# A chunked RWKV-7 recurrence on TensorE: half-array products per head made into full-array products for both heads

## The chip, the cores and the metric

The kernel runs on one core of a Trainium2 chip, in fp32. The metric is device time in microseconds (us) for one execution; lower is better. The engines are named as in the profile: PE (TensorE, matrix products; PEld is its weight load), DVE (VectorE), ACT (ScalarE), POOL (GpSimd) and SP (SyncE, which issues most transfers).

## The reference, cut to what matters

One decoder layer over 512 prompt tokens and 8 decode rows, model width 2048. A combined input projection feeds a gMLP branch and an RWKV-7 branch; both are gated, projected, merged and projected out. The part that the change touches is the recurrence of 32 heads of size 64:

```python
def step(s, inp):
    r_t, w_t, k_t, v_t, a_t, b_t = inp
    sa = jnp.einsum('bhij,bhj->bhi', s, a_t)
    s = s * w_t[:, :, None, :] + sa[..., None] * b_t[:, :, None, :] + v_t[..., None] * k_t[:, :, None, :]
    y_t = jnp.einsum('bhij,bhj->bhi', s, r_t)
    return s, y_t
...
proj = jnp.einsum('btd,de->bte', h, w_in)
...
s_new, y = _wkv_scan(wkv0, r_h, w_h, k_h, v_h, -kk, kk * a_h)
```

The kernel computes it in 8 chunks of 64 tokens: inside a chunk everything is matrix products and the inverse of a triangular 64 x 64 matrix, and the 64 x 64 state of each head goes from chunk to chunk.

## The kernel before, in words

**Main stream.** `emit_pe` writes one long stream of products of 128 x 128 weights with 260 columns: each addend pair costs three PE instructions (`acc<-hh,hi`, `acc<-hl,hi`, `acc<-hh,lo`), since weights and activations are split in a high and a low part. After each such triple it calls `side.tick()`, and there the side work may put in its own instructions. I call the place after a triple a slot.

**Side work.** Every instruction passes through the wrapper `Engine.call`, so all rows carry its line, L130, and are told apart by their tiles. `Side` holds generators. A planner (`Engine.cost`) estimates each engine's clock, and a bare `yield` means "go on when what this step started should be done, at the next slot". So the order on every engine is fixed when the program is built; on the chip, semaphores make an engine wait where the estimate was too short. `side.drain(t)` advances the planner without main products until task t is done.

**A pair of heads.** There are 16 pairs (two heads: partitions 0 to 63 and 64 to 127). The main stream has three or four input-projection jobs a pair, plus one more job in even pairs, 9 jobs (288 slots) in two pairs. `pair_task(p)` starts when k of pair p has been projected, and makes the token factors (`GGt`, `LK`), the products `gram`, the inverses of 32 x 32 blocks on POOL (tile `mtm`), and then the 64 x 64 inverses `MT`. `pair_aux(p)` makes `TK` (transposed factors) and `X` (token-major v, with room for the state). Then comes the chain of 8 chunks, one pair at a time (`lock["chain"]`), and a group norm. `pre_pair(p)` drains task p - 4 before pair p is projected.

**A chunk.** In lines 1086 to 1126, with h the head: product `R` (two products with 64 output partitions, K = 128), the part of `y` from X (two), a copy `rs` on DVE, product `U` with the inverse (two, K = 64), two copies into X on DVE, product `S` (two) and the second part of `y` (two, K = 64), then two adds on DVE that make the next state in X. An fp32 product is two PE instructions, so a chunk is 20 PE instructions in three groups: R with y, U, and S with y.

**The inverse.** Lines 1031 to 1080: blocks go from POOL through a DRAM tile (`md`) into `MT`, a fresh tile for each pair, with SP's transfers; a yield of 4500 ns; two DVE transposes (`m11tb`); the products `t` and `m`; copies; then the chain may begin.

Of the kernel before, what the change touches and what calls it, by code (L numbers as in the profile page):

```python
# [9 lines left out]
OP = mybir.AluOpType  # L10
# [86 lines left out]
class Both:  # L97
    """Two tiles indexed as one along their second dimension."""
# [8 lines left out]
class Engine:  # L107
    """An engine whose instructions are counted on the estimated clock."""
# [57 lines left out]
def hybrid_step(ctx, tc, xT, cT, wc, vecs, sst, win, wlr, w2a2, stw, lnv, wsT, w00, bs, pa, pb, wo,  # L166
# [7 lines left out]
    # ---------------------------------------------------------------- pools  # L174
# [49 lines left out]
    # ---------------------------------------------------------------- constants  # L224
# [4 lines left out]
    c9 = C((128, KD, 9), "c9")  # L229
    SY.dma_start(out=vec, in_=vecs)  # L230
    SY.dma_start(out=c9, in_=cT)

    open_pool("h", "h", "right")
    hs = slots("h", 32)
    open_pool("g", "gel")
    NG_S = 21
    gs = slots("g", NG_S)
    lp = open_pool("lead", "lead")
    xt = [hs(name="x") for _ in range(KD - 1)] + [lp.tile([128, N], F32, name="x15")]
# [22 lines left out]
    bones = C((128, 128), "bones")  # L262
# [3 lines left out]
    vmat = C((128, 128), "vmat")  # L266
    V.tensor_scalar(vmat, bones, 1.0 / 64, None, OP.mult)
    cmat = C((128, 128), "cmat")
# [29 lines left out]
    cpad = C((128, KD, 32), "cpad")  # L298
# [130 lines left out]
    # ---------------------------------------------------------------- conditioning, norm, h  # L429
# [26 lines left out]
    def cond_pair(g0, g1, tile_of, tmp, c0=0, w=256, kt=0):  # L456
        """w columns of c @ w_c + b_c from each of two column groups, features on partitions."""
# [73 lines left out]
    # ---------------------------------------------------------------- gMLP branch  # L531
# [219 lines left out]
    # ---------------------------------------------------------------- RWKV branch  # L751
    NW_S = 39
    ws = slots("wkv", NW_S)
    lora = {}
    pair = [dict() for _ in range(HP)]
# [5 lines left out]
    def pre_rwkv():  # L761
        side.drain(mix_task["g"])
        cur["gm"].release()
        cur["g"].release()
        open_pool("wkv", "wkv")
        load_lora(0)
# [61 lines left out]

    def parts(t):
        """The two addends of t that the tensor engine takes in one pass each."""  # L830
# [5 lines left out]
    def pair_aux(p):  # L836
        """What the chunks need besides the inverses: token-major v, b and k; the bonus; decode columns."""
# [43 lines left out]
        X = [ws((128, NCH, 64), name="x") for _ in range(2)]  # L881
        for cg in range(2):
# [3 lines left out]
            for c in range(4):  # L886
                o = 4 * cg + c
                if o < 7:
                    PE.transpose(ps[:, 128 * c:128 * c + 128], v[:, 64 * o:64 * o + 128], ident)
                    continue  # L890
                for h in range(2):
                    t = 64 * (7 * h)
                    PE.matmul(p3[hx[1 - h], c, 64 * h:64 * h + 64], v[hx[h], t:t + 64],
                              ident[hx[h], 64 * h:64 * h + 64], start=True, stop=True)
            yield
            A.copy(X[1][hx[0], 4 * cg:4 * cg + 4, :], p3[hx[0], :, 64:128])
            n = 4 - cg
            A.copy(X[0][hx[1], 4 * cg + 1:4 * cg + 1 + n, :], p3[hx[1], 0:n, 0:64])
            if cg:
                A.copy(X[0][hx[1], 0, :], p3[hx[1], 3, 0:64])  # L900
            give()
            yield
        for h in range(2):
            V.memset(X[h][hx[h], 0, :], 0.0)
# [3 lines left out]
    def pair_task(p):  # L908
# [5 lines left out]
        # squared norm of kk, decay, in-context rate  # L914
# [55 lines left out]
        del inv, f  # L970
        yield
        # token factors, scaled by the cumulated decay
        GGt = [[ws((128, 4, 128), name="gg") for _ in range(2)] for _ in range(2)]
# [6 lines left out]
        for cg in range(2):  # L980
            cc = slice(4 * cg, 4 * cg + 4)
            for h in range(2):
                x = hx[h]
                gg = GGt[h][cg]
                V.scalar_tensor_tensor(gg[x, :, 0:64], c3(k)[x, cc], vec[x, V_KK + p:V_KK + p + 1], pt[x, cc, 0:64],
                                       OP.mult, OP.mult)
                V.tensor_tensor(gg[x, :, 64:128], c3(r)[x, cc], pt[x, cc, 1:65], OP.mult)
# [5 lines left out]
            for c in range(4):  # L993
                for h in range(2):
                    PE.matmul(gr[h][:, 128 * c:128 * c + 128], LK[cg][hx[h], c, :], GGt[h][cg][hx[h], c, :],
# [12 lines left out]
            for h in range(2):  # L1008
                y = hx[1 - h]
                V.tensor_tensor(GGt[h][cg][y], g3[h][y], mask[y].unsqueeze(1).to_broadcast([64, 4, 128]), OP.mult)  # L1010
                give()
        del ip, pt
        aux = side.add(pair_aux(p))
        # inverses of the 32 x 32 diagonal blocks, one block on four partitions
# [28 lines left out]
        for h in range(2):  # L1043
            z = slice(64 * h, 64 * h + 32)
            V.transpose(M11[z], MT[z, :, 0:32])
# [19 lines left out]
        for c in range(NCH):  # L1065
            for h in range(2):
                z, y = slice(64 * h, 64 * h + 32), slice(64 * h + 32, 64 * h + 64)
                PE.matmul(p3[z, c, :], tb[y, c, :], MT[y, c, 32:64], start=True, stop=True)
# [3 lines left out]
        for h in range(2):  # L1072
            z = slice(64 * h, 64 * h + 32)
            V.tensor_copy(MT[z, :, 32:64], p3[z])
# [5 lines left out]
        del LK  # L1080
        # the chunks, one after another
# [4 lines left out]
        for c in range(NCH):  # L1086
            cg, c4 = c // 4, c % 4
            R = psum("ch", 1, "R")
            for h in range(2):
                PE.matmul(R[hx[h], 0:64], GGt[h][cg][:, c4, 0:64], X[h][:, c, :], start=True, stop=True)  # L1090
            for h in range(2):
                PE.matmul(py[hx[h], 64 * c:64 * c + 64], X[h][:, c, :], GGt[h][cg][:, c4, 64:128],
                          start=True, stop=False)
            if c:
                sp = wk.tile([128, 64], F32, tag="sp", bufs=2, name="sp")
                for h in range(2):
                    A.activation(sp[hx[h]], X[h][hx[h], c, :], AF.Identity, scale=pc[hx[h], c, :])
            yield
            rs = wk.tile([128, 64], F32, tag="rs", bufs=2, name="rs")
            V.tensor_copy(rs, R[:, 0:64])  # L1100
            yield
            U = psum("ch", 1, "U")
            for h in range(2):
                PE.matmul(U[hx[h], 0:64], MT[hx[h], c, :], rs[hx[h]], start=True, stop=True)
            yield
            for h in range(2):
                V.tensor_copy(X[h][hx[h], c, :], U[hx[h], 0:64])
            yield
            S = psum("ch", 1, "S")
            for h in range(2):  # L1110
# [5 lines left out]
            if c == NCH - 1:  # L1116
                sf = wk.tile([128, 64], F32, tag="sf", bufs=1, name="sf")
                V.tensor_tensor(sf, S[:, 0:64], sp, OP.add)
                G.dma_start(out=wkvp[p], in_=sf)
            else:  # L1120
                for h in range(2):
                    if c:
                        V.tensor_tensor(X[h][hx[h], c + 1, :], S[hx[h], 0:64], sp[hx[h]], OP.add)
                    else:
                        V.tensor_copy(X[h][hx[h], c + 1, :], S[hx[h], 0:64])
            yield
        lock["chain"] = None
        del X, GGt, BB, TK, MT
        # group norm
# [91 lines left out]
    # ---------------------------------------------------------------- decode rows of the WKV state  # L1221
    def sample_task():
# [71 lines left out]
        bc = lambda t, n: t.unsqueeze(2).to_broadcast([128, HP, n])  # noqa: E731  # L1294
# [18 lines left out]
    # ---------------------------------------------------------------- merge  # L1313
# [5 lines left out]
    def load_ya():  # L1319
        """All of y_a is loaded, and the tiles for which the slots suffice split, before the merge begins."""  # L1320
# [20 lines left out]
    def load_yb():  # L1341
# [7 lines left out]
        for p in range(HP):  # L1349
# [4 lines left out]
            hi, lo = ws(dt=F32R, name="ybh"), ws(dt=F32R, name="ybl")  # L1354
# [63 lines left out]
    # ---------------------------------------------------------------- output projection, residual, final norm  # L1418
# [176 lines left out]
```

## Time and profile before

| what | us |
|---|---|
| median of 3 runs (2405.62 to 2407.21) | 2406.22 |
| span of the profiled execution | 2405.5 |
| PE busy | 2365.4 (98%) |
| DVE busy | 1445.9 (60%) |
| ACT busy | 936.8 (39%) |
| POOL busy | 572.0 (24%) |

The profiled execution is told by its span, which lies 0.7 us under the median of the runs; the profile gives nothing else around it. PE products overlap in their pipeline, so the busy time of a group of them is no price: what a product costs the stream is read from the starts of its neighbours.

### The profile page before, as it was taken

The page shows a single profiled execution, that of the slowest core. Times are in us where ns is not written, and L with a number is a line of the kernel's source. Part 1 is how long each engine was busy: PE and PEld are TensorE (multiplying, and loading weights), DVE is VectorE, ACT ScalarE, POOL GpSimd, SP SyncE. Part 2 cuts the span into 40 slices and gives each one's busy share as a digit, 9 for nine tenths or more (in the row PEclk, how much of TensorE's full clock was granted, in tenths as well). Part 3 has the DMA queues.
Part 4 walks back from the last instruction along what each step waited for, and adds up shares of the span by engine and source line. Part 5 has one row for each costly group of instructions (what it writes and reads, how often), then busy time and mean ns, then how long its engine had stood idle before and what let it go on. Part 6 is the DMA issues. An engine that isn't in the chain of part 4 may idle for free.

```text
span 2405.5 us, 54026 instructions
## 1 busy us (share of the span) xinstructions
PE 2365.4 (98%) x22155; PEld 2222.8 (92%) x22155; DVE 1445.9 (60%) x3091; ACT 936.8 (39%) x2033; POOL 572.0 (24%) x1371
## 2 busy tenths in 40 slices
PE   8999999999999999999999999999999999999997
PEld 6899999999889989999899998998989999999996
DVE  6655452337667757776677666776678753434435
ACT  4333421243434454454544444444423342223333
POOL 3410011004322343323423244233512150000001
PEclk9999999999999999999999999999999999999998
DMA  8764267322222222222223232222234654334235
GB/s 291 278 228 150 97 209 244 104 94 88 89 86 83 85 75 88 87 75 84 83 80 96 66 92 79 85 87 68 96 127 162 215 187 137 119 120 172 88 97 142
DMA packets 165544, 296.73 MB, mean 123 GB/s; under 512 B 69192, under 2 KB 86344, under 8 KB 164656
## 3 DMA queue, kind: packets, MB, share of 16 engines
q1 hardware_dynamic: 149616, 239.13, 32.1%
q0 software_dynamic: 15680, 54.16, 6.1%
q8 instruction: 173, 2.83, 0.5%
q14 instruction: 75, 0.61, 0.1%
HBM read 264.94 MB, written 28.28 MB: 122 GB/s over the span
## 4 chain that ended last, share of the span: by engine, by line
PE 93%; issue 2%; POOL 2%; DMA 1%; DVE 1%; ACT 0%; SPq 0%; DVEq 0%; POOLq 0%; ACTq 0%
PE acc L130 77%; PE y L130 2%; PE m L130 2%; PE gram L130 2%; PE R L130 1%; PE S L130 1%; PE U L130 1%; POOL mtm L130 1%; PE lora L130 1%; PE vT L130 1%; DMA wcr<-in_wc 1%; PE tk L130 1%; PE t L130 0%; PE bon L130 0%; PE gnv L130 0%
## 5 line engine op out<-in xcount | busy, mean ns | idle before, releaser
L130 PE MATMUL acc<-hh,hi 128*128 128x260 f32 (+1 forms) x3904 | 1164.3, 298 | 2.9 <-DVE gel L130 1.8
L130 PE MATMUL acc<-hl,hi 128*128 128x260 f32 (+1 forms) x3904 | 1105.0, 283 | 0.3 <-DVE hl L130 0.3
L130 PE MATMUL acc<-hh,lo 128*128 128x260 f32 (+1 forms) x3904 | 1104.2, 283 | 0.4 <-DVE lo L130 0.4
L130 PEld LDWEIGHTS acc<-hh,hi 128*128 128x128 f32 (+1 forms) x3904 | 735.2, 188 | 48.3 <-issue 10.9
L130 PEld LDWEIGHTS acc<-hl,hi 128*128 128x128 f32 (+1 forms) x3904 | 736.5, 189 | 2.0 <-DVE hl L130 0.6
L130 PEld LDWEIGHTS acc<-hh,lo 128*128 128x128 f32 (+1 forms) x3904 | 735.8, 188 | 0.6 <-DVE lo L130 0.6
L130 DVE TENSOR_TENSOR lo<-raw,hi 128x512 fp32r<-128x512 f32 (+2 forms) x682 | 474.2, 703 | 269.6 <-ACT hi L130 265.7
L130 ACT CAST hi<-raw 128x512 fp32r<-128x512 f32 (+2 forms) x692 | 402.4, 597 | 305.9 <-PE acc L130 289.8
L130 POOL TENSOR_TENSOR mtm<-xm,mtm 128x60 f32<-128x60 f32 (+24 forms) x496 | 168.5, 340 | 223.4 <-DMA xm<-xd 187.3
L130 POOL TENSOR_TENSOR mtm<-mtm 128x60 f32<-128x60 f32 (+24 forms) x496 | 170.7, 344 | 38.8
L130 ACT ACTIVATE sp<-x,pc 64x64 f32<-64x64 f32 x224 | 77.3, 345 | 177.5 <-DVE x L130 175.1
L130 PE MATMUL acc<-mh,hi 128*128 128x260 f32 x512 | 144.8, 283 | 0.0
L130 PE MATMUL acc<-ybh,hi 128*128 128x260 f32 x512 | 144.8, 283 | 0.0
L130 PE MATMUL acc<-ybl,hi 128*128 128x260 f32 x512 | 144.6, 282 | 0.0
L130 PE MATMUL acc<-ybh,lo 128*128 128x260 f32 x512 | 144.6, 282 | 0.0
L130 PE MATMUL acc<-ml,hi 128*128 128x260 f32 x512 | 144.4, 282 | 0.0
L130 PE MATMUL acc<-mh,lo 128*128 128x260 f32 x512 | 144.2, 282 | 0.0
L130 DVE TENSOR_TENSOR gel<-gel,acc 128x260 f32<-128x260 f32 x160 | 65.2, 421 | 76.5 <-PE acc L130 76.0
L130 POOL DMA_DIRECT2D out<-xo x4 | 3.1, 771 | 421.2 <-DVE gs L130 413.4
L130 PEld LDWEIGHTS acc<-mh,lo 128*128 128x128 f32 x512 | 96.4, 188 | 0.0
L130 PEld LDWEIGHTS acc<-ybl,hi 128*128 128x128 f32 x512 | 96.4, 188 | 0.0
L130 PEld LDWEIGHTS acc<-mh,hi 128*128 128x128 f32 x512 | 96.4, 188 | 0.0
(281 smaller groups left out, 3330.0 us busy)
## 6 DMA issues: line engine op xcount, KB each, us to landing
raw<-in_win SPq DMA_DIRECT2D x240, 512.0 KB, 3.8
wcr<-in_wc POOLq DMA_DIRECT2D x57, 512.0 KB, 8.0
raw<-in_wo SPq DMA_DIRECT2D x38, 512.0 KB, 3.7
wcg<-in_wc SPq DMA_DIRECT2D x64, 256.0 KB, 5.5
raw<-in_pb SPq DMA_DIRECT2D x32, 512.0 KB, 3.8
xm<-xd SPq DMA_DIRECT2D x64, 128.0 KB, 2.7
raw<-in_pa SPq DMA_DIRECT2D x16, 512.0 KB, 3.7
x<-in_xT SPq DMA_DIRECT2D x16, 260.0 KB, 5.2
```

Of the source, the lines that this page charges most:

```text
L130: return f(*a, **k)
```

## The change

Only the recurrence and what feeds it are changed; comments are dropped, and a few constant tiles (`c9`, `cpad`, `bones`, `vmat`, `cmat`) move from the constant pool to pools that are released early.

- `GGt` (one tile for each head and half) becomes `GG` (one for each half, both heads side by side), `X` likewise holds both heads side by side, and `MT` is one 128 x 128 block-diagonal matrix for a chunk, in one tile for all pairs, zeroed once.
- R, U and S are one full-array product each. R and S have 128 columns, of which the diagonal 64 x 64 blocks are read; U has 64 columns.
- `rs` is two DVE copies, not one. U goes to a new tile `xu`, whose other half is copied from X on POOL twice every four chunks.
- The y products are held back and issued for four chunks together.
- GG waits until the chain of pair p - 2 is done, and the loads of MT until that of pair p - 1 is (`chain_passed`). Slots: `NW_S` 39 to 31, and five double-width tiles (tag D).
- The transposes of v take the first and last chunk together (`ends`), so that no half-array product remains there.

```diff
+    def wide(name, dt=F32, n=1024):
+        return cur["wkv"].tile([128, 2 * N], dt, tag="D", bufs=5, name=name)[:, 0:n]
+    def chain_passed(p):
+        while chain["done"] <= p:
+            yield "t"
...
+        yield from chain_passed(p - 2)
+        GG = [wide("gg").rearrange("p (c q h t) -> p c q h t", c=4, q=2, h=2) for _ in range(2)]
...
-        MT = ws((128, NCH, 64), name="MT")
+        yield from chain_passed(p - 1)
+        MT = chain["mt"]
         for q in range(4):
-            SY.dma_start(out=MT[32 * q:32 * q + 32, :, 32 * (q % 2):32 * (q % 2) + 32],
+            SY.dma_start(out=MT[32 * q:32 * q + 32, :, 32 * q:32 * q + 32],
                          in_=md[8 * q:8 * q + 8].rearrange("c j t -> j c t"))
-        for h in range(2):
-            V.memset(MT[64 * h + 32:64 * h + 64, :, 0:32], 0.0)
         yield 4500.0
...
+            if c4 == 0:
+                xu = ws((128, 4, 2, 64), name="xu")
+                for h in range(2):
+                    G.tensor_copy(xu[hx[1 - h], :, h, :], x[hx[1 - h], :, h, :])
             R = psum("ch", 1, "R")
-            for h in range(2):
-                PE.matmul(R[hx[h], 0:64], GGt[h][cg][:, c4, 0:64], X[h][:, c, :], start=True, stop=True)
-            for h in range(2):
-                PE.matmul(py[hx[h], 64 * c:64 * c + 64], X[h][:, c, :], GGt[h][cg][:, c4, 64:128],
-                          start=True, stop=False)
+            PE.matmul(R[:, 0:128], GG[cg][:, c4, 0], x[:, c4], start=True, stop=True)
...
-            V.tensor_copy(rs, R[:, 0:64])
+            for h in range(2):
+                V.tensor_copy(rs[hx[h]], R[hx[h], 64 * h:64 * h + 64])
...
-            for h in range(2):
-                PE.matmul(U[hx[h], 0:64], MT[hx[h], c, :], rs[hx[h]], start=True, stop=True)
+            PE.matmul(U[:, 0:64], MT[:, c, :], rs, start=True, stop=True)
...
-            for h in range(2):
-                PE.matmul(S[hx[h], 0:64], TK[cg][:, c4, 64 * h:64 * h + 64], X[h][:, c, :], start=True, stop=True)
-            for h in range(2):
-                PE.matmul(py[hx[h], 64 * c:64 * c + 64], X[h][hx[h], c, :], BB[cg][hx[h], c4, 64:128],
-                          start=False, stop=True)
+            PE.matmul(S[:, 0:128], TK[cg][:, c4, :], xu[:, c4], start=True, stop=True)
...
+            if c4 == 3:
+                for i in range(4):
+                    for h in range(2):
+                        PE.matmul(py[hx[h], 64 * (4 * cg + i):64 * (4 * cg + i) + 64], x[:, i, h, :],
+                                  GG[cg][:, i, 1, h, :], start=(c == 3 and i == 0), stop=False)
+                for i in range(4):
+                    for h in range(2):
+                        PE.matmul(py[hx[h], 64 * (4 * cg + i):64 * (4 * cg + i) + 64], xu[hx[h], i, h, :],
+                                  BB[cg][hx[h], i, 64:128], start=False, stop=(c == NCH - 1 and i == 3))
+        chain["done"] = p + 1
```

## Rows read from the trace of the kernel before

**Rows 1.** The page, parts 1 and 2: busy time of each engine with its share of the span and its instructions, and the granted clock of PE in 40 slices (9 is 90% or more of full speed).
```profile
PE 2365.4 (98%) x22155; PEld 2222.8 (92%) x22155; DVE 1445.9 (60%) x3091; ACT 936.8 (39%) x2033; POOL 572.0 (24%) x1371
...
PEclk9999999999999999999999999999999999999998
```

**Rows 2.** Busy time of each engine in a stretch of two pairs (us; the clock is the granted one).
```profile
910.50:1062.70 152.20, 152.20 (x1465) 137.95 (x1464) 105.74 (x245) 70.94 (x164) 52.05 (x145) 1.00 0.28 83
```

**Rows 3.** Timeline of PE around the three groups of a chunk: start and duration in us, what it writes and reads, how many instructions.
```profile
1000.05 0.28 PE L130 MATMUL acc<-hh,lo 128*128 128x260 f32 x1
1000.26 0.33 PE L130 MATMUL U<-rs,MT 64*64 64x64 f32 x4
1000.53 0.39 PE L130 MATMUL acc<-hh,hi 128*128 128x260 f32 x1
1000.75 0.28 PE L130 MATMUL acc<-hl,hi 128*128 128x260 f32 x1
...
1001.95 0.28 PE L130 MATMUL acc<-hh,lo 128*128 128x260 f32 x1
1002.16 0.34 PE L130 MATMUL S<-x,tk 128*64 128x64 f32 x4
1002.42 0.33 PE L130 MATMUL y<-bb,x 64*64 64x64 f32 x4
1002.68 0.39 PE L130 MATMUL acc<-hh,hi 128*128 128x260 f32 x1
1002.91 0.29 PE L130 MATMUL acc<-hl,hi 128*128 128x260 f32 x1
1003.03 0.29 PE L130 MATMUL acc<-hh,lo 128*128 128x260 f32 x1
...
1006.26 0.28 PE L130 MATMUL acc<-hh,lo 128*128 128x260 f32 x1
1006.48 0.34 PE L130 MATMUL R<-x,gg 128*64 128x64 f32 x4
1006.64 0.29 PE L130 MATMUL y<-gg,x 128*64 128x64 f32 x4
1006.86 0.39 PE L130 MATMUL acc<-hh,hi 128*128 128x260 f32 x1
1007.08 0.28 PE L130 MATMUL acc<-hl,hi 128*128 128x260 f32 x1
```

**Rows 4.** Timeline of PE earlier, in the gMLP branch, around one full-array fp32 product of 128 columns (tile mix; two instructions).
```profile
337.90 0.28 PE L130 MATMUL acc<-hh,lo 128*128 128x260 f32 x1
338.02 0.38 PE L130 MATMUL mix<-wst,vt 128*128 128x128 f32 x2
338.16 0.37 PE L130 MATMUL acc<-hh,hi 128*128 128x260 f32 x1
338.37 0.28 PE L130 MATMUL acc<-hl,hi 128*128 128x260 f32 x1
```

**Rows 5.** Groups of PE instructions over the whole span, by shape: count, then busy us and mean ns of one, then idle time before them.
```profile
L130 PE MATMUL R<-x,gg 128*64 128x64 f32 x512 | 43.1, 247 | 0.0
...
L130 PE MATMUL vT<-ident,sh 64*64 64x64 f32 x64 | 5.3, 243 | 0.0
```

**Rows 6.** Timelines of PE and of DVE in a chunk whose steps follow at the least distance, two slots.
```profile
1020.58 0.33 PE L130 MATMUL U<-rs,MT 64*64 64x64 f32 x4
1021.75 0.34 PE L130 MATMUL S<-x,tk 128*64 128x64 f32 x4
...
1021.02 0.47 DVE L130 COPY x<-U 64x64 f32<-64x64 f32 x2 [1.15 <-PE U L130]
```

**Rows 7.** Timelines of PE, SP, DVE, POOL and ACT: first R and last S of the chains of pairs 4 and 5, the load of pair 5's MT and its use, the last instruction of task 5, and the last evacuation before pair 9 is projected. Last, from the list of transfers, the median time from issue to landing (us) of the loads of MT.
```profile
909.70 0.34 PE L130 MATMUL R<-x,gg 128*64 128x64 f32 x4
...
975.75 0.34 PE L130 MATMUL S<-x,tk 128*64 128x64 f32 x4
...
975.39 1.82 SPq L130 DMA_DIRECT2D MT<-md  x4
...
985.63 0.89 DVE L130 STREAM_TRANSPOSE m11tb<-MT 32x256 f32<-32x256 f32 x2
...
996.74 0.34 PE L130 MATMUL R<-x,gg 128*64 128x64 f32 x4
...
1043.76 0.34 PE L130 MATMUL S<-x,tk 128*64 128x64 f32 x4
...
1074.70 0.56 POOL L130 DMA_DIRECT2D yb<-yc  x1 [2.05 <-DVE yc L130]
...
1144.89 0.39 ACT L130 ACTIVATE zth<-acc 128x260 f32<-128x260 f32 x1 [1.04 <-PE acc L130]
...
MT<-md SPq DMA_DIRECT2D x64, 32.0 KB, 1.9
```

**Rows 8.** PE's waits on the transposes of MT (us in total, times, longest), and two prices: the copy rs on DVE and a copy on POOL (count, busy us and mean ns of one, idle time before).
```profile
PE t L130 <- DVE m11tb L130: 3.6, 2, 3.4
...
L130 DVE COPY rs<-R 128x64 f32<-128x64 f32 x16 | 3.6, 223 | 4.1 <-PE R L130 4.0
...
L130 POOL COPY mtm<-inv 128x256 f32<-128x256 f32 x16 | 8.1, 508 | 2.1 <-DMA md<-mtm 2.1
```

More of the change, by code (lines that the diff above doesn't have):

```diff
@@ L228, in hybrid_step @@
     vec = C((128, V_N), "vec")
-    c9 = C((128, KD, 9), "c9")
     SY.dma_start(out=vec, in_=vecs)
-    SY.dma_start(out=c9, in_=cT)
     open_pool("h", "h", "right")
     hs = slots("h", 32)
-    open_pool("g", "gel")
+    gelp = open_pool("g", "gel")
     NG_S = 21
     gs = slots("g", NG_S)
+    cpad = gelp.tile([128, KD, 32], F32, name="cpad")
     lp = open_pool("lead", "lead")
+    c9 = lp.tile([128, KD, 9], F32, name="c9")
+    SY.dma_start(out=c9, in_=cT)
     xt = [hs(name="x") for _ in range(KD - 1)] + [lp.tile([128, N], F32, name="x15")]
@@ L261, in hybrid_step @@
     V.memset(ones, 1.0)
-    bones = C((128, 128), "bones")
+    bones = lp.tile([128, 128], F32, name="bones")
     V.memset(bones, 0.0)
@@ L749, in hybrid_step @@
         job(win[16 + m], 16, 128, mov_h, evac_z(m))
-    NW_S = 39
+    NW_S = 31
     ws = slots("wkv", NW_S)
     lora = {}
+    chain = {"done": 0}
     pair = [dict() for _ in range(HP)]
@@ L765, in pre_rwkv @@
         open_pool("wkv", "wkv")
+        chain["mt"] = wide("MT").rearrange("p (c t) -> p c t", c=NCH)
+        V.memset(chain["mt"], 0.0)
         load_lora(0)
@@ L880, in pair_aux @@
         collected.add(p)
-        X = [ws((128, NCH, 64), name="x") for _ in range(2)]
+        X = [ws((128, 4, 2, 64), name="x") for _ in range(2)]
+        ends = cur["wkv"].tile([128, 2, 64], F32, tag="ends", bufs=1, name="ends")
+        A.copy(ends, c3(v)[:, ::-7, :])
         for cg in range(2):
@@ L887, in pair_aux @@
                 o = 4 * cg + c
-                if o < 7:
-                    PE.transpose(ps[:, 128 * c:128 * c + 128], v[:, 64 * o:64 * o + 128], ident)
-                    continue
-                for h in range(2):
-                    t = 64 * (7 * h)
-                    PE.matmul(p3[hx[1 - h], c, 64 * h:64 * h + 64], v[hx[h], t:t + 64],
-                              ident[hx[h], 64 * h:64 * h + 64], start=True, stop=True)
-            yield
[L896 to L900, printed above, removed]
+                PE.transpose(ps[:, 128 * c:128 * c + 128],
+                             v[:, 64 * o:64 * o + 128] if o < 7 else ends.rearrange("p a b -> p (a b)"), ident)
+            yield
+            A.copy(X[cg][hx[0], :, 1, :], p3[hx[0], :, 64:128])
+            A.copy(X[cg][hx[1], 1:4, 0, :], p3[hx[1], 0:3, 0:64])
+            A.copy(X[1 - cg][hx[1], 0, 0, :], p3[hx[1], 3, 0:64])
             give()
@@ L903, in pair_aux @@
         for h in range(2):
-            V.memset(X[h][hx[h], 0, :], 0.0)
+            V.memset(X[0][hx[h], 0, h, :], 0.0)
         d["X"] = X
@@ L969, in pair_task @@
         d["b"], d["k2"] = b, k2
-        del inv, f
+        del inv, f, thw, g, tha
         yield
-        GGt = [[ws((128, 4, 128), name="gg") for _ in range(2)] for _ in range(2)]
+        yield from chain_passed(p - 2)
+        GG = [wide("gg").rearrange("p (c q h t) -> p c q h t", c=4, q=2, h=2) for _ in range(2)]
         LK = [ws((128, 4, 128), name="lk") for _ in range(2)]
@@ L1009, in pair_task @@
                 y = hx[1 - h]
-                V.tensor_tensor(GGt[h][cg][y], g3[h][y], mask[y].unsqueeze(1).to_broadcast([64, 4, 128]), OP.mult)
+                V.tensor_tensor(GG[cg][y, :, :, h, :], g3[h][y].rearrange("p c (q t) -> p c q t", q=2),
+                                mask[y].rearrange("p (q t) -> p q t", q=2).unsqueeze(1).to_broadcast([64, 4, 2, 64]),
+                                OP.mult)
                 give()
-        del ip, pt
+        del ip, pt, gg, r, k, b, k2, LK
         aux = side.add(pair_aux(p))
@@ L1044, in pair_task @@
             z = slice(64 * h, 64 * h + 32)
-            V.transpose(M11[z], MT[z, :, 0:32])
+            V.transpose(M11[z], MT[z, :, 64 * h:64 * h + 32])
         yield
@@ L1067, in pair_task @@
                 z, y = slice(64 * h, 64 * h + 32), slice(64 * h + 32, 64 * h + 64)
-                PE.matmul(p3[z, c, :], tb[y, c, :], MT[y, c, 32:64], start=True, stop=True)
+                PE.matmul(p3[z, c, :], tb[y, c, :], MT[y, c, 64 * h + 32:64 * h + 64], start=True, stop=True)
             if c == SPLIT:
@@ L1079, in pair_task @@
         X, TK = d.pop("X"), d.pop("TK")
-        del LK
         while lock["chain"] is not None:
@@ L1115, in pair_task @@
-            yield
[L1116 to L1125, printed above, removed]
@@ L1126, in pair_task @@
-            yield
+                o = S[hx[h], 64 * h:64 * h + 64]
+                if c == NCH - 1:
+                    if h == 0:
+                        sf = wk.tile([128, 64], F32, tag="sf", bufs=1, name="sf")
+                    V.tensor_tensor(sf[hx[h]], o, sp[hx[h]], OP.add)
+                elif c:
+                    V.tensor_tensor(X[(c + 1) // 4][hx[h], (c + 1) % 4, h, :], o, sp[hx[h]], OP.add)
+                else:
+                    V.tensor_copy(x[hx[h], 1, h, :], o)
+            if c == NCH - 1:
+                G.dma_start(out=wkvp[p], in_=sf)
@@ L1353, in load_yb @@
             yield 1500.0
-            hi, lo = ws(dt=F32R, name="ybh"), ws(dt=F32R, name="ybl")
+            if p < 5:
+                w = wide("ybw", F32R, 2 * N)
+                hi, lo = w[:, 0:N], w[:, N:2 * N]
+            else:
+                hi, lo = ws(dt=F32R, name="ybh"), ws(dt=F32R, name="ybl")
             A.copy(hi, t)
```

23 lines of the change are left out of this document (12 added, 11 removed).

## The prediction

> **What bounds the kernel now.** I read the page first: PE is busy for 98% of the span at full clock in almost every slice, DVE 60%, POOL 24% [rows 1]. Then I read the stretch of two pairs, where the change lives: PE is busy for all of its 152.20 us, DVE for 105.74, ACT for 70.94, POOL for 52.05 [rows 2]. So PE sets the pace, and what counts is how far apart the chain's products push the main products. The busy time of a group of products cannot be used, since they overlap; the starts can. The timeline gives them [rows 3]: two main products that follow each other start 0.12 us apart (1002.91, 1003.03). Where side products stand between, I take the distance from the last main product before to the second one after (the first one after still carries part of the delay) and subtract two plain steps, 0.24 us. That is the price of a group.
>
> **Prices before** [rows 3]. U: 1000.05 to 1000.75 is 0.70, so 0.46 for four small instructions. R with y: 1006.26 to 1007.08 is 0.82, so 0.58 for eight. S with y: 1001.95 to 1002.91 is 0.96, so 0.72 for eight of two shapes. Together 1.76 us a chunk; R has 512 instructions, four a chunk, so there are 128 chunks [rows 5], and the chain costs PE 225.3 us. These prices also show where the time goes. Four more instructions of the same shape add 0.58 - 0.46 = 0.12; four more of another shape (128 rows, then 64 rows) add 0.72 - 0.46 = 0.26. So of U's 0.46 only 0.12 is the products, and 0.34 is going from full-array to small products and back.
>
> **Prices after.** Before has a full-array fp32 product of 128 columns amid main products, mix [rows 4]: 337.90 to 338.37 is 0.47, so 0.23 for its two instructions, with no going over and back. R and S are this form exactly. U has the same weights and half the columns; no row has it, so I bound it by 0.12 (half) and 0.23, and take 0.23, because the same 128 x 128 weights have to be loaded twice. A chunk's three products then cost 0.69, and 128 of them 88.3 us. The y products stay small, 32 instructions for four chunks, 16 of each shape: the first four 0.46, twelve more of that shape 0.36, four of the other shape 0.26, twelve more 0.36, in sum 1.44 us, and 32 such batches 46.1 us. No row shows so long a batch; its upper bound is each further four at 0.26, 0.84 us more a batch or 27 us in all. The chain then costs 134.4 us, 90.9 less than before.
>
> The transposes of v: 64 small instructions [rows 5], four a pair, fall away, and one full transpose a pair takes their place. At U's 0.46 against one pass like half a mix product, 0.11, this is 0.35 a pair and 5.5 us. The sum for PE is 96.4 us: span 2405.5 - 96.4 = 2309.1.
>
> **A rule that speaks against it.** The rows price the full array at 0.23 against 0.12 for two small products inside a run of small ones. The Trainium skill, TensorEngine Tiling (Array Packing), section Theoretical Speedup, says that splitting the array pays up to 2x where a dimension is 64 or less, which is what before does and the change undoes. By that rule alone R, U and S would each be dearer by 0.11. The same page, section Key Properties, says that changing the tiling mode drains the engine; the trace agrees with this, and 0.34 is what it shows for one way in and out. I take the rows' sum; the other is a rival below.
>
> **What is given back on PE.** The order is fixed by the planner, which goes by slots, so the chain's steps keep about their distance in slots while the products between get shorter. In the tightest steps U at 1020.58 is followed by S at 1021.75, two slots later; the copies of U ran from 1021.02 to 1021.49, so S had 0.26 us to spare [rows 6]. U and S shrink to 0.23 each, which takes 0.46 - 0.23 = 0.23 from that step: it just fits, or waits some hundredths. For R the second copy rs, 0.22 more [rows 8], comes on top of 0.58 - 0.23 = 0.35, though the planner knows of the copy and may leave another slot. Bounds: nothing, or 0.1 us in each of some nine such steps a pair, 14 us. I take 5, since most steps are longer than two slots.
>
> **DVE, POOL, ACT.** One copy more a chunk is 128 x 0.22 = 28 us on DVE, less the 32 memsets of MT that go, 7 us at the copy's price. In two pairs that makes DVE about 108 us out of some 140: still under PE. The four copies a pair on POOL are 64 x 0.51 = 33 us by the nearest copy [rows 8], on an engine with two thirds of its time free [rows 2]. They stand behind inverse steps in POOL's queue, and S of chunks 0 and 4 needs them; R, rs, U and U's copies come first and cover some 2 us (U to S alone is 1.17 [rows 6]). If that cover is gone each costs up to 1 us, in the planner's slots rather than in stalls. Costed at nothing. The moved constants and the memset of MT stand outside this stretch or happen once: nothing.
>
> **The new waits.** GG waits for the chain of pair p - 2 and MT for that of p - 1. Before, MT of pair 5 was loaded from 975.39, while chain 4's last S stood at 975.75, and DVE transposed it only at 985.63 [rows 7]. After, the four loads go into SP's queue behind chain 4's end: 1.8 us of issue and 1.9 to land make about 980.5 with a us for the last adds, 5 us before use. Behind them on SP are weight loads, which before already waited longer behind the write of md. What is late next: if the chain ends 5 us later against the inverse, the transposes wait on DVE, and products t behind them on PE. Before shows two such waits, 3.6 us together, the longest 3.4 [rows 8]. Bounds: nothing, or 3.4 in each of 15 pairs, 51 us; nearest to the rows is a small part of it, and I take 0.6 a pair, 9 us.
>
> Is the chain itself fast enough? Chain 4 lasted 975.75 - 909.70 = 66.1 us, chain 5 1043.76 - 996.74 = 47.0 [rows 7], 56.5 on average. After, the least gap between chains is issue and landing of MT, 3.7, and from its transposes to the first R, 996.74 - 985.63 = 11.1, so 14.8. The second rs adds 8 x 0.22 = 1.8, the POOL copies about 2, and eight chunks lose 0.7 us of products each, 5.7. The cycle is 56.5 + 14.8 + 1.8 + 2 - 5.7 = 69.4 us. The main stream gives a pair every 76.1 - 96.4/16 = 70.1. It fits barely, so I forecast no queue of chains.
>
> **The sum:** 2309.1 + 5 + 9 = 2323.1 for the span, with 0.7 around it 2323.8 against the median of 2406.22.
>
> **Rivals.**
>
> *All is hidden.* No step waits, MT always lands in time, and U costs half: 2309.1 + 0.7 = 2309.8, or 14 us less with U at 0.12, 2296. For it: before, PE hardly ever waits in this stretch. Against it: that 0.26 us to spare is used up.
>
> *The chain falls behind.* If the cycle is longer than 70.1 us, chains fall back pair by pair. Main products stall when task p is not done as pair p + 4 begins. Task 5's last instruction stands at 1074.70 and pair 9 begins at about 1144.9 [rows 7], so 70 us can be used up, 4.7 a pair over 15 pairs. A cycle of 77 would cost 15 x 6.9 - 70 = 34 us, and DVE and PE would wait on MT in every pair, up to 51 us: 2345 to 2405. For it: 69.4 against 70.1 is close, and even chains are 66 us long. Against it: the long chains are long because they wait for other work at the planner's leisure.
>
> *The chain becomes the bound, and the kernel slower.* The same mechanism, from the point where it costs more than 97 us: a cycle above 70.1 + (70 + 97)/15 = 81.2 us, so 12 more than I work out. At 83 the time is about 2434. It would need chains longer by a fifth; nothing in rows 7 shows that.
>
> *The small products were the cheaper form.* By the tiling rule: if going over and back were not what the 0.34 is, and the interruption cost the same with full-array products, the three would be dearer by 128 x 3 x 0.11 = 42 us: 2448. The mix row speaks against it, since it is an interruption too and costs 0.23 in all [rows 4].
>
> **Chances and range.** My forecast (2308 to 2345) 0.62; all hidden (below 2308) 0.13; the chain falls behind (2345 to 2401) 0.17, of which the last bit, 0.02, counts as no change; slower by the chain 0.05; slower by the small products 0.03. No measurement of this kernel tells less than 0.2%, 5 us, from no change. So faster 0.90, same 0.02, slower 0.08. The range leaves out the lower half of the hidden case (0.06), the upper third of the chain's (0.06) and both slower ones (0.08): 2302 to 2385.
>
> **What would show it.** In the trace after: R, U and S with 128 rows and 128 columns, 256 instructions each, and main products 0.47 us apart around a lone R; y in runs of 32, near 1.7 us from main to second main; two pairs in about 140 us; DVE's transposes of MT at times waiting for its load; PE's waits on DVE in the chain, some 15 us where there were almost none. I am wrong if PE's busy rows show other prices, or if the time between two R of chunk 0 is more than two pairs' main products take, with PE idle at the start of a pair.

## The result

The changed kernel takes 2346.66 us (median of 4 runs, 2345.44 to 2347.86), the kernel before in the same series 2405.92 (2404.52 to 2407.21): ratio 0.9756, 95% interval 0.9743 to 0.977. The forecast was faster, and the range 2302 to 2385 holds the time; the likeliest value, 2323.8, is 23 us too low. So some 59 us came of 82 forecast, and the question is where the other 23 are.

The page after, parts 1, 2 and 4 (the last is the chain that ended last, by engine), against [rows 1]:
```profile
PE 2294.7 (98%) x21339; PEld 2212.8 (94%) x21339; DVE 1481.9 (63%) x3204; ACT 944.3 (40%) x2065; POOL 612.0 (26%) x1435
...
PEclk9999999999999999999999999999999999999998
...
PE 85%; DVE 6%; issue 5%; DMA 2%; POOL 2%; ACT 1%; SPq 0%; DVEq 0%; POOLq 0%; ACTq 0%
```
Two stretches of two pairs, against [rows 2] (us; busy time of PE, PEld, DVE, ACT, POOL; granted clock):
```profile
1186.10:1330.90 144.80, 143.43 (x1363) 137.24 (x1363) 109.80 (x256) 71.70 (x168) 57.56 (x153) 1.00 0.28 85
1330.90:1475.60 144.70, 143.31 (x1363) 137.06 (x1362) 110.99 (x260) 71.71 (x168) 57.91 (x153) 1.00 0.30 87
```
Two pairs take 144.75 us (144.5 on average from first R to first R), not the 140 forecast and not the 152.2 of before. And PE, which was busy for all of the stretch before, now has 1.4 us of holes in each.

Timelines of PE around a lone S and around a batch of y, against [rows 3]:
```profile
1306.05 0.28 PE L130 MATMUL acc<-hh,lo 128*128 128x260 f32 x1
1306.17 0.38 PE L130 MATMUL S<-xu,tk 128*128 128x128 f32 x2
1306.31 0.37 PE L130 MATMUL acc<-hh,hi 128*128 128x260 f32 x1
1306.51 0.29 PE L130 MATMUL acc<-hl,hi 128*128 128x260 f32 x1
...
1366.56 0.28 PE L130 MATMUL acc<-hh,lo 128*128 128x260 f32 x1
1366.77 0.69 PE L130 MATMUL y<-gg,x 128*64 128x64 f32 x16
1367.39 0.68 PE L130 MATMUL y<-bb,xu 64*64 64x64 f32 x16
1368.00 0.39 PE L130 MATMUL acc<-hh,hi 128*128 128x260 f32 x1
1368.22 0.28 PE L130 MATMUL acc<-hl,hi 128*128 128x260 f32 x1
```
From main to second main, less 0.24: S 0.46 - 0.24 = 0.22, the batch 1.66 - 0.24 = 1.42. These are the prices forecast (0.23 and 1.44). So the prices are right where nothing waits. PE's waits now have rows for the chain that before had none (us in total, times, longest), and the one on MT's transposes against [rows 8]:
```profile
PE U L130 <- DVE rs L130: 7.3, 13, 1.1
...
PE R L130 <- DVE x L130: 1.7, 3, 1.2
PE S L130 <- DVE xu L130: 1.5, 8, 0.2
...
PE t L130 <- DVE m11tb L130: 0.4, 2, 0.2
```
The rows of waits hold only the holes that show between modelled ends, 10.5 us. Starts say more. Two main products start 0.12 apart though each is drawn 0.28 long, so a start that comes 0.15 late leaves no hole. I took, for each R, U and S, its start less the start before it less the plain step (0.12; ahead of the small products of before 0.21), and added up what is over 0.02 us. Before, that is 0.1 us in the whole span. After, it is 7.0 for R (36 of 128), 14.0 for U (50) and 8.1 for S (61): 29.2 us in 147 late starts.

The longest show where they come from. PE, then DVE, around a U:
```profile
1228.14 0.38 PE L130 MATMUL R<-x,gg 128*128 128x128 f32 x2
...
1228.96 0.28 PE L130 MATMUL acc<-hh,lo 128*128 128x260 f32 x1
1230.29 0.41 PE L130 MATMUL U<-rs,MT 128*128 128x64 f32 x2 [1.05 <-DVE rs L130]
...
1228.57 1.22 DVE L130 TENSOR_TENSOR_SCAN cs<-smask,thw 128x512 f32<-128x512 f32 x1
1229.71 0.43 DVE L130 COPY rs<-R 64x64 f32<-64x64 f32 x2
```
R is done early enough, but DVE is in a scan, the two copies rs stand behind it, and U, whose turn in PE's queue was 1229.08, waits until 1230.29; all of PE's queue waits with it. The planner's formula for DVE, 80 + 1.04 ns an element, prices the scan at 612 ns, lo at 612 and a copy of 64 columns at 147; in the trace they take 1238, 717 and 220. By what DVE did just ahead of the copies, the late starts over 0.1 us (83 cases, 25.6 us) are 7.5 us behind a lo (25 cases), 6.5 behind a scan (10), the rest scattered over DVE's other instructions; in only 5 cases was DVE idle just before.

A product that waits loses more than the wait. PE's weight loads and products around an S that waited (the S of 1306.17 above, which did not, had its load at 1306.06):
```profile
1310.36 0.28 PE L130 MATMUL acc<-hh,lo 128*128 128x260 f32 x1
1310.83 0.46 PE L130 MATMUL S<-xu,tk 128*128 128x128 f32 x2 [0.19 <-DVE xu L130]
1311.04 0.36 PE L130 MATMUL acc<-hh,hi 128*128 128x260 f32 x1
1311.24 0.28 PE L130 MATMUL acc<-hl,hi 128*128 128x260 f32 x1
...
1310.80 0.30 PEld L130 LDWEIGHTS S<-xu,tk 128*128 128x128 f32 x2 [0.36 <-PE acc L130]
```
The weights (tk, long there) are loaded only after the wait, 0.03 us ahead of the product instead of 0.11, and from S to the second main product it is 0.41 instead of 0.34. Over all R, U and S that stand alone between main products, the median of this distance is 0.42 for the 133 late ones and 0.34 for the others. The Trainium skill, TensorE: Matmul & The Clock Gate, section Step-by-step: what each phase is for, says that weight loads are pulled ahead of products in flight; the S of 1306.17 agrees, the waiting S shows none of it.

### The profile page after: what moved, and what is told of

It reads as the page before. It is cut to its first block, busy times and chain, and to the rows that moved or that the text cites. A ratio compares the mean times of both kernels' runs of the same rounds, so it can differ in the third digit from the quotient of the medians.

```text
span 2346.0 us, 52985 instructions
## 1 busy us (share of the span) xinstructions
PE 2294.7 (98%) x21339; PEld 2212.8 (94%) x21339; DVE 1481.9 (63%) x3204; ACT 944.3 (40%) x2065; POOL 612.0 (26%) x1435
## 4 chain that ended last, share of the span: by engine, by line
PE 85%; DVE 6%; issue 5%; DMA 2%; POOL 2%; ACT 1%; SPq 0%; DVEq 0%; POOLq 0%; ACTq 0%
PE acc L130 71%; PE gram L130 2%; PE y L130 2%; PE m L130 2%; PE S L130 1%; PE R L130 1%; PE U L130 1%; DMA wcr<-in_wc 1%; DVE lo L130 1%; PE lora L130 1%; POOL mtm L130 1%; PE tk L130 1%; DVE cs L130 1%; DVE inv L130 1%; POOL x L130 0%
## 5 line engine op out<-in xcount | busy, mean ns | idle before, releaser
L130 POOL TENSOR_TENSOR mtm<-xm,mtm 128x60 f32<-128x60 f32 (+24 forms) x496 | 173.3, 349 | 190.5 <-DMA xm<-xd 155.5
L130 POOL TENSOR_TENSOR mtm<-mtm 128x60 f32<-128x60 f32 (+24 forms) x496 | 179.5, 362 | 38.9
L130 PE MATMUL acc<-ybl,hi 128*128 128x260 f32 x352 | 99.5, 283 | 0.0
L130 PE MATMUL acc<-ybh,hi 128*128 128x260 f32 x352 | 99.4, 282 | 0.0
L130 PE MATMUL acc<-ybh,lo 128*128 128x260 f32 x352 | 99.0, 281 | 0.0
L130 PEld LDWEIGHTS acc<-ml,hi 128*128 128x128 f32 x512 | 96.4, 188 | 0.0
```

Of the source, the lines that this page charges most:

```text
L130: return f(*a, **k)
```

## The experiments

The theory after the result: the waits of R, U and S on DVE, with these late loads, are what the forecast lacked, some 40 us. Rivals: the array form costs more than its lone price, VectorE is short whatever the chain does, or the chain is too slow for the pairs. In the diffs, the lines with + are the experiment's. Medians are held against 2346.7 for the changed kernel; brackets are the ratio to the kernel before with its 95% interval.

**The chain without its waits, first try (chain_unwaited).** Products read a constant, and the three results have columns of their own in one bank; `plan` tells the planner the old operand, so that the order stays.
```diff
+        ch = psum("ch", 1, "ch")
...
-            R = psum("ch", 1, "R")
-            PE.matmul(R[:, 0:128], GG[cg][:, c4, 0], x[:, c4], start=True, stop=True)
+            R = ch[:, 0:128]
+            PE.matmul(R, GG[cg][:, c4, 0], ident, start=True, stop=True, plan=[x])
```


> The changed kernel in which R, U and S read a constant 128x128 array as their moving operand instead of x, rs and xu, each from its own columns of one PSUM bank; the copies on the vector engine, the y products, the number of products, their shapes and their order are those of the changed kernel. So the state recurrence is left out, and no product of the chain waits for a copy. Theory (the vector engine's queue, longer than the planner's prices, makes the chain's products wait on TensorE): the starts lost in the changed kernel add up to 29 us, and each product that waited also lost some 0.1 us because its weights were loaded only after the wait: 30 to 40 us faster than the changed kernel, 2307 to 2317 us. Rival 1 (the array-shaped products simply cost more than the 0.23 us I took): the same products at the same places cost the same, 2340 to 2347. Rival 2 (VectorE is short in any case, and a TensorE that doesn't wait here waits for the operands of the main products instead): 2330 to 2347, with waits for lo in the place of those for rs, x and xu.

Measured: 2342.61 [0.9742, 0.9727 to 0.9756]. This settles nothing: the products still waited for the copies out of the one bank that all three write (6.6 us on rs in the rows of waits, against 7.3; late starts 21.9 us), though U now reads nothing of rs and writes other columns than rs reads. What it shows is that sharing one tile in one bank is enough to keep the wait.

**The chain without its waits (chain_apart).** Now the copies do not read the bank either.
```diff
-                V.tensor_copy(rs[hx[h]], R[hx[h], 64 * h:64 * h + 64])
+                V.tensor_copy(rs[hx[h]], ident[hx[h], 64 * h:64 * h + 64], plan=[R])
-            PE.matmul(U[:, 0:64], MT[:, c, :], rs, start=True, stop=True)
+            PE.matmul(U[:, 0:64], MT[:, c, :], ident[:, 0:64], start=True, stop=True, plan=[rs])
```


> The changed kernel in which TensorE and VectorE no longer meet in the recurrence: R, U and S read a constant 128x128 array as their moving operand, and the copies and adds behind them read the same constant instead of R, U and S. Count, shape and order of the products and copies are those of the changed kernel; the state recurrence is left out. In the run before this one R, U and S still waited, since they wrote a bank that the copies had yet to read; here neither engine waits for the other. Theory (the waits of R, U and S for VectorE, 29 us of late starts and some 0.1 us more for each product that waited, are what the forecast missed): 30 to 40 us under the changed kernel, 2307 to 2317 us, with the price of a lone S at 0.23 instead of 0.32 us. Rival 1 (the array-shaped products, or what stands around them, cost more than I took): 2335 to 2347, with the prices as they were. Rival 2 (VectorE is short, and the main products wait for lo instead): 2325 to 2347, with a wait for lo of over 5 us.

Measured: 2307.05 [0.9597, 0.9583 to 0.9611], 39.6 us under the changed kernel. No start of R, U or S is late, a lone one costs 0.22 each, and the two stretches of two pairs, in the same columns:
```profile
1168.30:1308.20 139.90, 139.90 (x1360) 135.63 (x1359) 109.20 (x259) 71.27 (x169) 57.77 (x152) 1.00 0.30 90
1308.20:1448.40 140.20, 140.20 (x1362) 135.92 (x1361) 110.06 (x259) 71.52 (x169) 59.01 (x153) 1.00 0.30 90
```
PE is busy for all of it, and two pairs take the 140 forecast. PE, DVE, ACT and POOL run the same instructions in the same order as in the changed kernel, and the waits for lo stay at 0.4 us, so VectorE is not short in itself; it is late for this chain. The theory holds, and 40 us is its size.

**The small products (chain_small).** R, U and S as two products of 64 output partitions each, y batched. The planner is told 110 ns for each of them, and the order on the engines is another than in the changed kernel.
```diff
-            PE.matmul(U[:, 0:64], MT[:, c, :], rs, start=True, stop=True)
+            for h in range(2):
+                PE.matmul(U[hx[h], 0:64], MT[hx[h], c, 64 * h:64 * h + 64], rs[hx[h]], start=True, stop=True)
```


> The changed kernel with R, U and S as two 64x64 products again (one for each head, no block-diagonal operand used), the y products still in batches of four chunks. Theory (by the rows of before a lone pair of small products costs 0.46 us, a lone array product 0.23): 3 x 0.23 x 128 = 88 us more work on TensorE than the changed kernel; what the waits for VectorE take now (30 to 40 us) may fall away as the steps lie further apart, so 48 to 88 us slower: 2395 to 2435. Rival 1 (the array form brought little, the gain of 59 us came from the batches of y): within 15 us of the changed kernel, 2347 to 2362. Rival 2 (small products are the cheaper form): faster than 2347.

Measured: 2396.26 [0.9969, 0.9958 to 0.9979], 50 us above the changed kernel. A lone one:
```profile
1304.22 0.28 PE L130 MATMUL acc<-hh,lo 128*128 128x260 f32 x1
1304.43 0.33 PE L130 MATMUL U<-rs,MT 64*64 64x64 f32 x4
1304.70 0.39 PE L130 MATMUL acc<-hh,hi 128*128 128x260 f32 x1
1304.92 0.28 PE L130 MATMUL acc<-hl,hi 128*128 128x260 f32 x1
```
That is 0.70 - 0.24 = 0.46, as before the change. The late starts fall to 4.9 us in 17. So 88 us of price less some 35 of waits (24 of late starts, 0.08 for each of 130 fewer late products) come to about the 50. The array form is worth 88 where nothing waits (this kernel is 89 us above chain_apart, with 5 of late starts in it), and the batches of y, with the transposes of v, only the 9 us that this kernel keeps over the one before (2404.93 in its series).

**y in every chunk (y_each_chunk).**
```diff
-            if c4 == 3:
-                for i in range(4):
+            for h in range(2):
+                PE.matmul(py[hx[h], 64 * c:64 * c + 64], x[:, c4, h, :], GG[cg][:, c4, 1, h, :],
+                          start=(c == 0), stop=False)
...
```


> The changed kernel with the four y products of each chunk issued behind S of that chunk, instead of 16 at every fourth chunk; array products as in the changed kernel. Theory: a run of small products costs 0.34 us once for going from the array's form to the small one and back, and little for each product; four runs of four in place of one of sixteen is three more such changes per four chunks: 3 x 0.34 x 32 = 33 us slower, 2375 to 2385 (2347 + 28 to 38). Rival 1 (price by product alone, no fixed part): no change, 2343 to 2351. Rival 2 (the y products behind S give VectorE the time that the next step needs, and the waits shrink by as much as the runs cost): 2345 to 2360.

Measured: 2449.87 [1.0188, 1.0173 to 1.0204], 103 us above the changed kernel, three times what I expected. A run of eight:
```profile
1302.19 0.28 PE L130 MATMUL acc<-hh,lo 128*128 128x260 f32 x1
1302.40 0.34 PE L130 MATMUL y<-gg,x 128*64 128x64 f32 x4
1302.66 0.33 PE L130 MATMUL y<-bb,xu 64*64 64x64 f32 x4
1302.92 0.39 PE L130 MATMUL acc<-hh,hi 128*128 128x260 f32 x1
1303.15 0.28 PE L130 MATMUL acc<-hl,hi 128*128 128x260 f32 x1
...
PE R L130 <- DVE x L130: 24.1, 27, 2.0
```
It costs 0.96 - 0.24 = 0.72, so 128 x 0.72 - 32 x 1.42 = 47 us; in the expectation I had left out the step from one shape to the other, which the prediction counts. Late starts rise from 29.2 to 58.1, most of it R: 29 us. Of the other 27, some 9 are 99 products of 260 columns that ran at a granted clock of 0.50, 0.22 us apart instead of 0.12 (8 in the changed kernel); the rest I have not traced.

**Two attempts to shorten the waits on VectorE.** One slot more in the ring, as a control for the runs with 32 slots (slot_more), then half of each copy on ScalarE (halves_two_engines; the diff shows R, and U likewise):
```diff
+                (A.copy if h else V.tensor_copy)(rs[hx[h]], R[hx[h], 64 * h:64 * h + 64])
```


> The changed kernel with one slot more in the ring of operand buffers (32 instead of 31; one rs instead of two, and one constant fewer, make the room). It is what the two kernels with 32 slots are to be held against. By every theory the slot alone changes little, 2340 to 2352; if it comes out above 2360, what those two lost was not the change made in them.

> The changed kernel with one slot more in the ring of operand buffers (32; room from a second rs and a constant), and with the copy of the second head's half of R and of U on ScalarE, the first staying on VectorE. Theory (VectorE's queue makes the products wait): each step needs one 0.22 us copy of VectorE instead of two, 2 x 128 x 0.22 = 56 us less work there; the waits fall by about half, 2325 to 2337. Rival (ScalarE's queue, with casts of 0.6 us each, is as late as VectorE's, and U and S then wait for the later of two engines): 2347 to 2365.

Measured: 2348.67 [0.9766, 0.9751 to 0.978] for the control, 2461.41 [1.0238, 1.0223 to 1.0253] for the halves. The control shows no change that can be told. The halves lose 113 us against it, far more than the rival said.

R copied in one piece (one_copy), and with the scan priced (one_copy_scan):
```diff
-            for h in range(2):
-                V.tensor_copy(rs[hx[h]], R[hx[h], 64 * h:64 * h + 64])
+            V.tensor_copy(rs, R[:, 0:128])
...
+            if op == "tensor_tensor_scan":
+                return 120 + 2.12 * n
```


> The changed kernel with R copied in one piece, 128x128, in place of two copies of 64x64, and U taken over all 128 columns (the inverse is block-diagonal, so the blocks that count come out the same). VectorE: two copies at 0.22 us become one at about 0.29 (0.22 and 64 more elements at about 1 ns), 0.15 us less before each U and 19 us less in all. TensorE: U has 128 columns like R, whose lone price is 0.23 as well: nothing. Theory (waits for VectorE): the 14 us that U starts late shrink by 0.1 us for each of the 50 late ones, and those behind it a little: 2336 to 2346. Rival (128 columns cost more than 64 on TensorE, some 0.1 us each): 2355 to 2360.

> The kernel with one copy of R, and the planner's price of the scan (cs) set from 0.61 to 1.2 us, as the trace has it; nothing else. Theory (steps that come due behind a scan are issued before the copy is done: 6.5 us of the late starts stand behind a scan): 5 to 8 us under the run with one copy alone, 2328 to 2340. Rival (the planner's order shifts elsewhere and gives it back): within 5 us of the run with one copy, or above it.

Measured: 2345.72 [0.9755, 0.9741 to 0.977], no change that can be told, and 2356.57 [0.9798, 0.9781 to 0.9814], 11 slower than that. With one copy the late starts of U fall from 14.0 to 1.7 us, but those of R rise from 7.0 to 10.2 and those of S from 8.1 to 14.7, of which 6.3 are two long waits. Ahead of the first, the S of 1080.93, DVE shows:
```profile
1078.61 1.23 DVE L130 TENSOR_TENSOR_SCAN cs<-smask,thw 128x512 f32<-128x512 f32 x1 [2.13 <-POOL coll_r L130]
```
The scan waits for a small copy on POOL, coll_r, and the copy of U stands behind it. The changed kernel has no such wait; one copy of R changes the order on the engines, and this comes with it. It is what the next runs turn on.

**Steps later.** By 200 ns (chain_later), by 50 ns for every step behind another engine (latency_225), and by 100 ns with one copy (one_copy_later):
```diff
-            yield
+            yield 200.0
```


> The changed kernel with one slot more in the ring of operand buffers (32 in place of 31; room from a second rs and a constant), and with the planner told to issue U, S and the next R 200 ns later than it thinks the copies done. Theory (the waits come from copies that end up to half a microsecond later than the planner thinks): 200 ns takes away the shorter waits and shortens the longer ones, between a third and two thirds of 30 to 40 us: 2320 to 2336. Rival 1 (the recurrence is then too slow for the rhythm of the pairs: 24 steps x 0.2 us or more on a cycle of 72 us): 2350 to 2380, with the gaps between the recurrences gone. Rival 2 (waits are not what holds the kernel): 2344 to 2350.

> The changed kernel with one number of the planner changed, the time from the end of one engine's instruction to the start of another's that reads it, from 175 to 225 ns. It delays every step that follows another engine's, the recurrence's by 2 x 50 ns for each product and its copies. Theory (the planner issues the recurrence's products before their operands are there): 2330 to 2343. Rival (the order shifts elsewhere and gives it back): 2347 to 2365.

> The kernel with one copy of R (2346), with the planner told to issue U, S and the next R 100 ns later than it thinks the copies done. Theory (waits of R, U and S for VectorE cost 40 us in the changed kernel; one copy shortens the chain by 0.15 us a step, which pays for part of the delay): the shorter waits, 0.1 us and the 0.1 us of a weight load that comes too late, fall away: 2325 to 2340. Rival (later steps push the pairs' cycle out, as 200 ns did): 2350 to 2375.

Measured: 2383.29 [0.9913, 0.9897 to 0.993], 2384.12 [0.9918, 0.99 to 0.9937] and 2380.23 [0.9901, 0.9885 to 0.9918], all 34 to 38 us slower than what they start from. I expected a chain too slow for the pairs if it went wrong. That is not what the trace shows: the gaps between chains are still there (12 to 23 us in chain_later, 13 to 23 in one_copy_later), and in one_copy_later the late starts of U are 28.7 us in five long waits. One of them, PE, then DVE, then POOL:
```profile
1398.04 0.79 PE L130 MATMUL U<-rs,MT 128*128 128x128 f32 x2 [5.58 <-DVE rs L130]
...
1399.50 0.42 PE L130 MATMUL acc<-hl,hi 128*128 128x260 f32 x1
1399.72 0.42 PE L130 MATMUL acc<-hh,lo 128*128 128x260 f32 x1
...
1395.98 1.23 DVE L130 TENSOR_TENSOR_SCAN cs<-smask,thw 128x512 f32<-128x512 f32 x1 [5.14 <-POOL coll_r L130]
1397.12 0.67 DVE L130 TENSOR_TENSOR lo<-raw,hi 128x512 fp32r<-128x512 f32 x1
1397.70 0.29 DVE L130 COPY rs<-R 128x128 f32<-128x128 f32 x1
...
1395.11 0.31 POOL L130 TENSOR_TENSOR mtm<-xm,mtm 128x70 f32<-128x70 f32 x1
...
1395.75 0.19 POOL L130 COPY coll_r<-sh 128x8 f32<-128x8 f32 x1
```
A copy of 0.19 us on POOL stands at the end of a run of inverse products; the scan on DVE waits for it, 5.14 us; rs stands behind the scan, and U behind rs. In the slower runs the same copy stands among the waits: on ScalarE for coll_r 28.9 us in chain_later, on VectorE 14.8 in latency_225 and 21.0 in one_copy_scan, on ScalarE 54 in the halves. In the changed kernel there is no wait for coll_r on either engine; its order happens to avoid it.

**That queue taken away (one_copy_later_coll).** One thing changed in one_copy_later:
```diff
-            G.tensor_copy(coll[n][:, p, :], t[:, T:N])
+            V.tensor_copy(coll[n][:, p, :], t[:, T:N])
```


> The run with one copy of R and steps 100 ns later (2380), with one thing changed: the five small copies of each pair into the collected columns (coll_r and the others, 128x8) on VectorE instead of GpSimd. In that run the scan cs on VectorE waited for the copy coll_r, which stood behind some twenty products of the doubled inverse on GpSimd; the copy rs stood behind the scan, and U behind the copy for 5.5 to 6 us in five of the sixteen pairs, after which TensorE's granted clock was 0.50 for some 6 us. Theory (that queue, and not the later steps, made the run slow): 29 us of waits and about 5 x 3 us of the slow clock go, VectorE gains 80 copies at about 0.15 us in its queue: 2328 to 2345. Rival (the later steps push the pairs' cycle out, as I expected of them): 2365 to 2380.

Measured: 2328.62 (2327.74 to 2330.55) [0.9687, 0.9668 to 0.9705], 52 us under the run it differs from in this one line, and 18 us under the changed kernel: the fastest kernel here that leaves nothing out. Late starts are 17.6 us, where that run had 48.3, and no wait for coll_r is left. So GpSimd's queue made that run slow, and not the later steps. What the later steps bring by themselves stays open: from the changed kernel this one differs by the one copy, the later steps and the five moved copies, and no run has the moved copies without the later steps. That chain_later, latency_225, one_copy_scan and the halves lost theirs the same way is argued from their rows of waits; no run of its own shows it, and it is not all: in the halves PE also waits 27.5 us once for DVE's say (8.4 in chain_later), work on the decode rows, a wait that the changed kernel does not have.

## Why the prediction was right, and what was mis-sized

*Prices on PE: right.* R, U and S at 0.23 where they do not wait (0.22 to 0.23), the batch 1.42 for 1.44, the transposes of v 0.34 less a pair (0.79 to 0.44) for 0.35. What the side products add to the main stream in all falls from 392.4 us before to 294.7 in chain_apart, 97.7 for the 96.4 summed, and its time of 2307.05 stands for my hidden case of 2309.8. U's lower bound of 0.12 is out.

*The tight steps: the term that failed.* I gave 5 us with a bound of 14, 0.1 us for each of nine steps a pair that come two slots apart. Measured, it is 336.2 - 294.7 = 41.5 us on PE: 29.2 of late starts, and the other 12.3 over 147 late products, 0.08 each, as the late loads above cost. Nine steps a pair are 144, so the number of late products was about right, but by luck: only some 70 of the 147, with 15 us, come two slots after the step before, and a late one costs 0.28 on average, not 0.1. Three errors of mine. I called the whole 0.26 us between copies and S in [rows 6] spare; in the trace after, the 83 products over 0.1 us late start 0.15 us (median) after the end of their copy, so only some 0.11 was spare, and taking 0.23 away makes that step 0.12 late with no queue at all. I took the copies as beginning as soon as PE is done, as they do in [rows 6], and looked only at the steps that are near in slots; but the copies wait in VectorE's queue behind lo, the scan and others. And I put VectorE down as under PE on its share (110 of 145 us here), which says nothing on how late one copy comes. Before, a step was longer by the 0.23 us and more that the small products took, and that was room which hid this; chain_small, with the small products back, has 4.9 us of late starts.

*The wait on MT: sized 9, measured 0.4* in the rows of waits. The chain's end did not push it; the rival with 51 us is out. So the 23 us are accounted for: 2307.05 for 2309.8, and 39.6 given back for the 14 that I took.

*The chain's cycle: right as far as shown.* In chain_apart PE is busy for all of two pairs and gives a pair each 70.0 us (70.1 forecast), so the main stream sets the pace. The gaps between the chains are about 15 and 18 us there, hardly more than the 14.8 that I took as the least, so they are no slack by themselves; but early pairs have gaps down to 12.1, so that least was too high. In the changed kernel it is PE with its waits that takes 72.4. So the time fell just past my forecast, which ended at 2345, into the band that I had given to "the chain falls behind", but not by that mechanism: that the range holds it is in part luck.

*VectorE and GpSimd:* DVE 109.8 and 111.0 us in two pairs for the 108 forecast; the POOL copies xu 64 at 0.49 us for 0.51.

*Small products the cheaper form: refuted* by chain_small. The Trainium skill, TensorEngine Tiling (Array Packing), section Key Properties, says that changing the tiling mode drains the engine; the prices agree with it, 0.46 for two small products that stand alone, 0.22 for the array product that takes their place.

## What to carry to other kernels

When a product on the critical engine gets shorter, ask what its length was hiding: here the copies of another engine, and nearly half of the 88 us was given back there. Size such waits from the queue ahead of the copy (what stands before it, how long by the trace, not by the planner's price), for every step and not only for the nearest ones, and count late starts instead of rows of waits. An engine with much free time can still hold the whole chain: five small copies a pair, behind a long run on GpSimd, cost 52 us when the order had changed.

## What the hardware showed beyond this

The long waits cost twice. Busy time of each engine around the wait above in one_copy_later, with the granted clock after POOL's column:
```profile
1392.00:1394.00 2.00, 0.47 (x4) 0.26 (x3) 0.00 (x0) 0.00 (x0) 1.61 (x6) 1.00 0.00 0
1394.00:1396.00 2.00, 0.00 (x0) 0.00 (x0) 0.02 (x1) 0.00 (x0) 1.69 (x7) 0.73 0.00 0
1396.00:1398.00 2.00, 0.00 (x0) 0.00 (x0) 2.00 (x4) 0.79 (x4) 1.84 (x3) 0.50 0.00 0
...
1400.00:1401.00 1.00, 1.00 (x6) 1.00 (x6) 0.42 (x1) 1.00 (x4) 0.79 (x3) 0.50 0.41 164
...
1402.00:1403.00 1.00, 1.00 (x11) 0.85 (x10) 0.00 (x0) 1.00 (x4) 0.82 (x3) 1.00 0.00 0
```
PE stood idle for 5.6 us; the granted clock went to 0.50, the 1.2 GHz level, while it stood, and was still there at 1401, so that main products started 0.22 us apart instead of 0.12 (1399.50, 1399.72). The short waits of the changed kernel leave it at 1.00, as in its two stretches above.
